# Tokens of a chunk laid out by residue modulo 16, and VectorE's 32x32 transpose for probability blocks of dilation 16 alone

## The chip, the cores and the metric

The kernel runs on one core of one Trainium2 chip. A core has five engines that each execute their own list of instructions in order: TensorE (PE in the profile, with its weight loads as PEld), VectorE (DVE), ScalarE (ACT), GpSimd (POOL) and SyncE (SP), and 16 DMA engines that move data between DRAM and on-chip memory. The metric is the device time of one execution in microseconds (us).

## The reference, cut to what matters

One decoder layer over 2048 tokens of width 1024, float32. Twelve attention heads of width 64 use a mixture of three dilated windows; two column groups of 128 go through a short gated convolution; both are concatenated, projected, normalised and added to the input.

```python
DILATED_PATTERNS = ((128, 1), (512, 4), (2048, 16))
h = rmsnorm(x, norm_pre_g)
q, k, v, g_attn, c_h, c_b, c_c, g_conv = jnp.split(h @ w_in, cuts, axis=-1)
q = rope(q, pos); k = rope(k, pos)
for window, dilation in DILATED_PATTERNS:      # keys at distance 0, d, 2d, ..., window
    o_i, lse_i = dilated_window_attn(q, k, v, window, dilation)
o = sum(softmax(lse over the three patterns) * o_i)
attn_out = o * silu(g_attn)
conv_out = c_b * causal_depthwise_conv(c_c * c_h, conv_w) * silu(g_conv)
x = x + rmsnorm(concat(attn_out, conv_out) @ w_out, norm_post_g)
```

A key that lies more than 512 tokens behind its query is seen by pattern 16 alone, so only if the distance is a multiple of 16.

## The kernel before, in words

**Tiles and stages.** The tokens are cut into four chunks of 512 (`C`). The projection's columns are eight groups of 512: group 0 and group 7 are the two convolution units, groups 1 to 6 the six head pairs. A unit is one group for one chunk, 32 units in the order group by group, chunk 0 to 3 in each. `x_chunk` (L416) loads a chunk of x (four tiles of 128 tokens by 1024), transposes it on PE (L442), splits it into a rounded float32r part and a remainder (L446, L448) and writes it to DRAM (L451); later groups read it back (`x_stream`, L475). A projection is three matmuls per 128x128x512 tile (L848 to L850). The last stage (L952 on) projects the concatenated result with w_out, reads x once more (L1043), adds, and stores (L1046).

**Order of tokens in a chunk.** Tile r of a chunk holds the tokens 4p + r, p from 0 to 127: the tokens are sorted by their residue modulo 4. So `x[rows[i]]` at L435, `x[t0, dl]` at L1043 and `out[t0, dl]` at L1046 step through DRAM by four rows, one row for each of 128 partitions.

**Attention.** `attn_unit` (L533) rotates k and q, keeps the keys of all chunks so far in `KK`, makes a second copy of q in token order (`Q1`, L582, on POOL), and transposes v on PE (L594). `v1`, the values in token order, is made through DRAM (L607, L610). Two sets of scores follow. Kind 4 (`score4`, L623) takes the patterns 4 and 16 together: for each residue r modulo 4 and each head of the pair, 128 queries against 128 keys of every chunk up to b. Kind 1 (`score1`, L648) takes pattern 1: 128 queries against 256 keys around them. VectorE adds a mask and takes the minimum (L638, L666), ScalarE exponentiates (L642, L670). `probs` (L677) takes up to four 128x128 blocks of probabilities, transposes them on PE (L684), copies them rounded from PSUM with ScalarE (L689), has VectorE form the remainder (L690), and multiplies them with the values (L703). Kind 4 of chunk b has 4(b+1) blocks for a head; of these the blocks of the chunks 0 to b-2 lie wholly more than 512 tokens back.

**Weights of the mixture.** Denominators of kind 1 go from E through DRAM into the order of kind 4 (L758, L760); the two weights are computed in small VectorE steps, squared up by one VectorE transpose (L785), written to DRAM (L788) and read back broadcast over partitions (L791). VectorE and POOL apply them (L807 to L810) and the result goes to `mix_d`.

**What sets the order.** Nothing is issued as it is written. Each operation is added to a planner (`Plan`, L111) with an engine, an assumed duration, a priority and what it reads and writes; `schedule` (L172) plays these through and fixes one static order for each engine. All DMAs go out through SP in that order. Buffers are rings of slots: five PSUM banks `st`, three `pt` slots for transposed probabilities, eight slots for x tiles, nine `xt` slots, six `xr` slots for the x rows of the last stage.

Of the kernel before, what the change touches and what calls it, by code (L numbers as in the profile page):

```python
# [40 lines left out]
def _constants():  # L42
# [9 lines left out]
    order = np.arange(C).reshape(128, 4).T.reshape(-1)  # L52
    rope[:, :, 0] = cs.transpose(1, 0, 2)[:, :, order]
    rope[:, :, 1] = sn.transpose(1, 0, 2)[:, :, order]
    q = np.arange(128)[:, None]
    k = np.arange(128)[None, :]
# [4 lines left out]
    tok = (np.arange(128) % 32) * 4 + np.arange(128) // 32  # L61
# [234 lines left out]
def hybrid_layer(ctx: ExitStack, tc: tile.TileContext, x, w_in, w_out, conv_w, g_pre, g_post,  # L296
# [27 lines left out]
    e_d = [dram.tile([4, 32, 4, 4], F32, name=f"ed{i}") for i in range(2)]  # L324
    a_d = [dram.tile([32, 4, 128], F32, name=f"ad{i}") for i in range(2)]
# [24 lines left out]
    KK = [ap_.tile([128, 4, NB * 128], F32R, name=f"kk{i}") for i in range(2)]  # L350
# [64 lines left out]

    def x_chunk(b):  # L416
# [6 lines left out]
        rows = [slice(b * C + i, (b + 1) * C, 4) for i in range(4)]  # L423
        if b == 0:

            for h in range(4):
                for g in range(2):
                    def load(h=h, g=g):
                        assert all(xn[2 * g + k].slot is xs_r[2 * g + k] for k in range(2))
                        nc.sync.dma_start(p4_r[g].ap.rearrange("p (i a) c -> p i (a c)", i=2)[:, :, h * 256:(h + 1) * 256],  # L430
                                          x[0:C].rearrange("(p i) d -> p i d", i=4)[:, 2 * g:2 * g + 2, h * 256:(h + 1) * 256])
                    add("DMA", dmat(256), -160 + 4 * h + g, load, w=[(xn[2 * g], h), (xn[2 * g + 1], h)], land=3.6)
# [62 lines left out]
    def conv_unit(n, i, b, zs):  # L495
# [16 lines left out]
        add("DVE", 0.25, pe, lambda: vec.tensor_copy(u.ap[:, 0:2, 1:], u.ap[:, 4:6, 0:127]), r=[(u, 1)], w=[(u, 2)])  # L512
# [20 lines left out]
    def attn_unit(n, p, b, zs):  # L533
# [3 lines left out]
        sl = slice(b * 128, (b + 1) * 128)  # L537

        def by_r(a):
            return a.rearrange("p (r i) -> p r i", r=4)  # L540
# [40 lines left out]
        for l in range(2):  # L581
            add("POOL", poolt(C) / 2, pr, lambda l=l: pool.tensor_copy(  # L582
                Q1.ap[:, l].rearrange("p (g r j) -> p g r j", g=4, r=4), Q.ap[:, l].rearrange("p (r g j) -> p g r j", g=4, r=4)),
                r=[(Q, l)], w=[(Q1, l)])
# [20 lines left out]
        d, dk = v_d[u % 2], ("vd", u % 2)  # L605
        for g in range(4):
            add("DMA", 0.5, pr, lambda g=g: nc.sync.dma_start(  # L607
                d[g].rearrange("(r j) c -> j r c", r=4), f(v2.ap[32 * g:32 * g + 32]).rearrange("j r k d -> j r (k d)")),
                r=[v2], w=[dk + (g,)], land=3.8)
        add("DMA", dmat(512), pr, lambda: nc.sync.dma_start(f(v1.ap), d.rearrange("g i c -> i g c")),  # L610
            r=[dk + (g,) for g in range(4)], w=[v1], land=5.0)
# [11 lines left out]
        def score4(r0):  # L623
# [3 lines left out]
            def qk():  # L627
                for r in range(r0, r0 + per):
                    for x, (i, j) in enumerate(products):
                        for h, (lo, hi) in enumerate(halves):  # L630
                            mm(ps[h].ap[:, (r - r0) * w:(r - r0 + 1) * w], Q.ap[lo:lo + 64, i, r * 128:(r + 1) * 128],  # L631
                               KK[j][lo:lo + 64, r, 0:w], start=x == 0, stop=x == 2)

# [14 lines left out]
        def score1(g0):  # L648
# [3 lines left out]
            def qk():  # L652
                for j, g in enumerate(lo):
                    k0 = b * 128 + (g - 1) * 32
# [22 lines left out]
        def probs(h, kind, blk, O):  # L677
            ps, pt = Tok(st_r), Tok(pt_r)
            m = len(blk)
            pp = P[h, kind]  # L680

            def tr():
                for i, (a, c) in enumerate(blk):
                    nc.tensor.transpose(ps.ap[:, i * 128:(i + 1) * 128], pp.ap[:, a, c * 128:(c + 1) * 128], ident)  # L684
            add("PE", 0.111 * m, pr, tr, r=[(pp, a) for a in sorted({a for a, _ in blk})] + ["cst"], w=[ps, (pt, "hold")])

            def p4():
                return ps.ap[:, :m * 128].rearrange("p (i c) -> p i c", c=128)
            add("ACT", actt(m * 128, True), pr + URG, lambda: act.copy(pt.ap[:, :m, 0, :], p4()), r=[ps], w=[(pt, 0)])  # L689
            add("DVE", dvet(m * 128), pr + URG, lambda: vec.tensor_tensor(  # L690
                pt.ap[:, :m, 1, :], p4(), f(pt.ap[:, :m, 0, :]), op=ALU.subtract), r=[ps, (pt, 0)], w=[(pt, 1)])

            def pv(part):
                for i, (a, c) in part:
                    dst = O[a // 2].ap.rearrange("p (l q) -> p l q", l=2)[:, :, (a % 2) * 128:(a % 2 + 1) * 128]
# [9 lines left out]
            for half in range(2):  # L705
                part = [(i, ac) for i, ac in enumerate(blk) if ac[0] // 2 == half]
                if part:
                    attn_last.append(add("PE", mmt(256) * len(part), pr, lambda part=part: pv(part), r=[(pt, 0), (pt, 1)] + vs, w=[O[half]]))
# [28 lines left out]
        for kind in (4, 1):  # L737
            for h in range(2):
# [7 lines left out]
                for i in range(0, len(bl), 4):  # L746
                    probs(h, kind, bl[i:i + 4], O)
# [12 lines left out]
        add("DMA", 0.5, pr, lambda: nc.sync.dma_start(  # L760
            X.ap.rearrange("p r c -> p (r c)"), ed.rearrange("g j r c -> (g j) (r c)")), r=[ek + (r,) for r in range(4)], w=[X], land=3.0)
# [14 lines left out]
        def w_b():  # L776
# [11 lines left out]
        add("DMA", 0.5, pr, lambda: nc.sync.dma_start(  # L788
            ad.rearrange("c g f -> g c f"), ar.ap.rearrange("p a b -> p (a b)")), r=[ar], w=[ak], land=2.0)
        for h in range(2):  # L790
            add("DMA", 0.73, pr, lambda h=h: nc.sync.dma_start(  # L791
                ab.ap[64 * h:64 * h + 64].rearrange("p i g f -> p (i g f)"),
                ad[2 * h:2 * h + 2].rearrange("i g f -> (i g f)").unsqueeze(0).to_broadcast([64, 1024])),
                r=[ak], w=[(ab, h)], land=8.0)


        def rows(t):
            return t.ap.rearrange("p (r g j) -> p g r j", r=4, g=4)

        def tokens(t):  # L800
            return t.ap.rearrange("p (g r j) -> p g r j", g=4, r=4)

        def weight(i):
            return ab.ap[:, i].rearrange("p g (r j) -> p g r j", r=4)

        a4, a1 = UU[4][0], UU[1][0]
        add("DVE", dvet(C), pr, lambda: vec.tensor_tensor(rows(a4), rows(a4), weight(1), op=ALU.mult), r=[ab], w=[a4], port=True)  # L807
        add("DVE", dvet(C), pr, lambda: vec.tensor_tensor(tokens(a1), tokens(a1), weight(0), op=ALU.mult), r=[ab], w=[a1], port=True)
# [306 lines left out]
```

## Time and profile before

| what | value |
|---|---|
| median of 3 runs | 1220.3 us (1217.9 to 1220.44) |
| the profiled execution | 1222.89 us |
| its span on the core | 1220.8 us |
| granted TensorE clock, mean | 0.994 |
| busy: PE, DVE, ACT, POOL | 1201.8, 916.0, 717.9, 260.1 us |
| DMA moved | 280.39 MB, 230 GB/s on average |

The span is the time from the first to the last instruction of the core; the execution's own time is 2.1 us longer. Engine busy times overlap each other. A row of the profile's groups gives line, engine, operation, output and input tile, shape, count, then the sum of busy time, the mean in ns of one, and the idle time just before it with what ended it. SPq rows are DMAs that SP issues; their duration is the issuing, not the transfer. A busy PE is one with a matmul in its pipeline: what one matmul costs is read from the distance between starts.

### The profile page before, as it was taken

The numbers are of one execution on the slowest core, as the hardware profiler recorded it, in microseconds if no ns is written. First come the engines' busy times: TensorE is split into PE (matmuls) and PEld (weight loads), VectorE is DVE, ScalarE is ACT, GpSimd is POOL, SyncE is SP. The second block draws the span as 40 slices with busy tenths as digits, with TensorE's granted clock in tenths as the row PEclk, the third lists the DMA queues.
The fourth block names the chain that finished last, engine by engine and source line by source line (L and its number), as shares of the span: only waits on it lengthen the run. The fifth ranks groups of instructions, "written<-read, shape, count | busy, mean of one in ns | idle before, by whom it ended". The sixth has DMA issues, their size and how long they took to land.

```text
span 1220.8 us, 20955 instructions
## 1 busy us (share of the span) xinstructions
PE 1201.8 (98%) x6856; PEld 993.4 (81%) x6856; DVE 916.0 (75%) x2287; ACT 717.9 (59%) x1874; POOL 260.1 (21%) x212
## 2 busy tenths in 40 slices
PE   8999999999999999999999999999999999999997
PEld 6888888888878888788887888788888888777886
DVE  5556477877777787787788867787877759988876
ACT  6533447767557676576667676486676553454443
POOL 0011123322322232222332223222323113000000
PEclk9999999999999999999999999999999999999999
DMA  9989777766777657766877748767678779555452
GB/s 342 343 317 338 269 232 236 234 205 200 240 252 245 205 182 261 240 184 209 260 223 254 243 119 269 232 234 248 199 233 280 213 229 302 174 163 175 136 181 86
DMA packets 155884, 280.39 MB, mean 230 GB/s; under 512 B 31872, under 2 KB 90368, under 8 KB 155776
## 3 DMA queue, kind: packets, MB, share of 16 engines
q1 hardware_dynamic: 155776, 279.06, 69.6%
q8 instruction: 54, 0.88, 0.3%
q14 instruction: 54, 0.44, 0.1%
HBM read 215.36 MB, written 51.05 MB: 218 GB/s over the span
## 4 chain that ended last, share of the span: by engine, by line
PE 84%; DVE 8%; DMA 3%; ACT 2%; issue 1%; SPq 1%; DVEq 0%; ACTq 0%
PE z L848 16%; PE z L850 16%; PE z L849 16%; PE st L703 8%; PE st L684 7%; PE st L631 4%; PE st L659 3%; PE st L1010 2%; PE st L1008 2%; PE st L1009 2%; DMA rp<-rp 1%; PE z L1008 1%; PE z L1010 1%; PE z L1009 1%; ACT p L642 1%
## 5 line engine op out<-in xcount | busy, mean ns | idle before, releaser
L848 PE MATMUL z<-xt,w 128*128 128x512 f32 x960 | 397.1, 414 | 0.0
L850 PE MATMUL z<-xt,w 128*128 128x512 f32 x960 | 377.7, 393 | 0.0
L849 PE MATMUL z<-xt,w 128*128 128x512 f32 x960 | 376.4, 392 | 0.0
L850 PEld LDWEIGHTS z<-xt,w 128*128 128x128 f32 x960 | 180.5, 188 | 40.3
L848 PEld LDWEIGHTS z<-xt,w 128*128 128x128 f32 x960 | 181.2, 189 | 32.7 <-issue 3.4
L849 PEld LDWEIGHTS z<-xt,w 128*128 128x128 f32 x960 | 181.5, 189 | 25.8
L690 DVE TENSOR_TENSOR pt<-st,pt 128x512 fp32r<-128x512 f32 x216 | 142.3, 679 | 48.1 <-ACT pt L689 46.2
L642 ACT ACTIVATE p<-p,sm 128x128 f32<-128x128 f32 (+3 forms) x192 | 105.9, 555 | 73.2 <-DVE sm L638 72.9
L689 ACT CAST pt<-st 128x512 fp32r<-128x512 f32 x216 | 120.0, 579 | 36.0 <-PE st L684 34.1
L703 PEld LDWEIGHTS st<-pt,v 128*128 128x128 f32 x852 | 121.5, 190 | 18.2 <-DVE pt L690 4.9
L703 PE MATMUL st<-pt,v 128*128 128x256 f32 x852 | 133.1, 287 | 2.0 <-DVE pt L690 1.9
L684 PE MATMUL st<-cst,p 128*128 128x128 f32 x852 | 123.1, 275 | 2.4 <-DVE sm L638 1.0
L723 DVE TENSOR_TENSOR uu<-st,uu 64x256 f32<-64x256 f32 x192 | 80.0, 421 | 57.1 <-ACT uu L722 53.5
L684 PEld LDWEIGHTS st<-cst,p 128*128 128x128 f32 x852 | 100.6, 141 | 22.8 <-issue 3.2
L752 POOL TENSOR_TENSOR uu<-uu 128x512 f32<-128x512 f32 x48 | 72.4, 1509 | 209.1 <-DVE uu L723 207.4
L638 DVE CUSTOM_DVE_ANT_0 p<-st,cst 128x128 f32<-128x128 f32 (+3 forms) x192 | 81.8, 487 | 46.7 <-PE st L631 46.4
L721 ACT COPY uu<-st 64x256 f32<-64x256 f32 x192 | 70.2, 368 | 58.7 <-PE st L703 52.3
L670 ACT ACTIVATE p<-p,e 128x256 f32<-128x256 f32 (+1 forms) x192 | 94.9, 499 | 12.4 <-DVE e L666 12.3
L562 POOL TENSOR_TENSOR rp<-rp,cs 128x512 f32<-128x512 f32 x24 | 35.3, 1472 | 225.7 <-DMA rp<-rp 145.4
L666 DVE CUSTOM_DVE_ANT_0 p<-st,cst 128x256 f32<-128x256 f32 (+1 forms) x192 | 66.8, 411 | 20.5 <-PE st L659 20.4
L562 DVE TENSOR_TENSOR rp<-rp,cs 128x512 f32<-128x512 f32 x72 | 55.9, 791 | 23.4 <-DMA rp<-rp 23.0
L722 ACT COPY uu<-st 64x256 f32<-64x256 f32 x192 | 69.6, 367 | 3.2 <-DVE uu L723 0.4
(320 smaller groups left out, 1842.7 us busy)
## 6 DMA issues: line engine op xcount, KB each, us to landing
xt<-xt SPq DMA_DIRECT2D x256, 512.0 KB
cs<-t SPq DMA_DIRECT2D x28, 768.0 KB
raw<-in_w_in SPq DMA_DIRECT2D x59, 256.0 KB
rp<-rp SPq DMA_DIRECT2D x192, 64.0 KB
vd<-v SPq DMA_DIRECT2D x96, 128.0 KB
v<-vd SPq DMA_DIRECT2D x24, 512.0 KB
ab<-ad SPq DMA_DIRECT2D x48, 256.0 KB
mix<-g SPq DMA_DIRECT2D x32, 256.0 KB
```

Source lines behind the costliest of these rows:

```text
L562: add(e, dur, pr, lambda o=o, a=a, i=i, eng=eng: eng.tensor_tensor(o.ap, a.ap, cs.ap[:, i], op=ALU.mult), r=[cs], w=[o], port=True)
L638: add("DVE", dvet(w) + 0.01, pr + URG, lambda h=h, r=r, P4=P4: vec.tensor_tensor_reduce(P4.ap[:, r, 0:w], ps[h].ap[:, (r - r0) * w:(r - r0 ...
L642: add("ACT", actt(w) + 0.19, pr, lambda h=h, r=r, P4=P4: act.activation(P4.ap[:, r, 0:w], P4.ap[:, r, 0:w], AF.Exp, bias=s4(0, h)[:, r:r + ...
L670: add("ACT", actt(256 - lo[g]) + 0.19, pr, lambda h=h, g=g, P1=P1: act.activation(P1.ap[:, g, lo[g]:], P1.ap[:, g, lo[g]:], AF.Exp, bias=E ...
L684: nc.tensor.transpose(ps.ap[:, i * 128:(i + 1) * 128], pp.ap[:, a, c * 128:(c + 1) * 128], ident)
L689: add("ACT", actt(m * 128, True), pr + URG, lambda: act.copy(pt.ap[:, :m, 0, :], p4()), r=[ps], w=[(pt, 0)])
L690: add("DVE", dvet(m * 128), pr + URG, lambda: vec.tensor_tensor(pt.ap[:, :m, 1, :], p4(), f(pt.ap[:, :m, 0, :]), op=ALU.subtract), r=[ps, ...
L703: mm(dst, v, pt.ap[:, i], start=s, stop=e)
L723: add("DVE", dvet(256), pr + URG, lambda: vec.tensor_tensor(cols(a, lo), o()[lo:lo + 64, 0], cols(a, lo), op=ALU.add), r=[O], w=[(a, (h, h ...
L848: mm(z.ap, w.ap[:, 0, js], xt.ap[:, 0], start=kt == 0, stop=False)
L849: mm(z.ap, w.ap[:, 0, js], xt.ap[:, 1], start=False, stop=False)
L850: mm(z.ap, w.ap[:, 1, js], xt.ap[:, 0], start=False, stop=kt == KT - 1)
```

## The change

Tile r of a chunk now holds the tokens 16a + 4s + r, at place 32s + a: within a tile the tokens are sorted by residue modulo 16, in four runs of 32. A 128x128 block of kind 4 that only pattern 16 sees then has its nonzero entries in four 32x32 squares on its diagonal. VectorE transposes such blocks in place in squares of 32 (`vec.transpose`), with no PE transpose and no PSUM bank; the ScalarE copy and VectorE remainder then read them from on-chip memory instead of PSUM. The blocks of the chunks b-1 and b go through PE as before.

All that depends on the order of tokens follows: the rope table, the masks, the reading of x, the stores of the result, the views of keys and queries, the convolution's shift (two copies where there was one), and the three detours through DRAM (v, E, the weights). Chunk 0 of x is loaded by 12 DMAs instead of 8, half of them issued by ScalarE's queue.

```diff
+    def by_place(t, b):
+        return t[b * C:(b + 1) * C].rearrange("(a s r) d -> r s a d", a=32, s=4)
...
-        rows = [slice(b * C + i, (b + 1) * C, 4) for i in range(4)]
+        rows = by_place(x, b)
...
-            for h in range(4):
-                for g in range(2):
-                    def load(h=h, g=g):
-                        nc.sync.dma_start(p4_r[g].ap.rearrange("p (i a) c -> p i (a c)", i=2)[:, :, h * 256:(h + 1) * 256],
-                                          x[0:C].rearrange("(p i) d -> p i d", i=4)[:, 2 * g:2 * g + 2, h * 256:(h + 1) * 256])
+            for h0, h1 in ((0, 1), (1, 2), (2, 4)):
+                for i, z in enumerate(xn):
+                    cols = slice(h0 * 256, h1 * 256)
+                    add("DMA", dmat(128 * (h1 - h0)), -160 + 4 * h0 + i / 2, lambda z=z, i=i, cols=cols: (act if i % 2 else nc.sync).dma_start(
+                        z.ap[:, cols], rows[i][:, :, cols]), w=[(z, h) for h in range(h0, h1)], land=3.6)
...
-                add("DMA", dmat(512), b * 100 - 160 + i, lambda z=z, i=i: nc.sync.dma_start(z.ap, x[rows[i]]), w=[(z, h) for h in range(4)])
+                add("DMA", dmat(512), b * 100 - 160 + i, lambda z=z, i=i: nc.sync.dma_start(z.ap, rows[i]), w=[(z, h) for h in range(4)])
...
-                               KK[j][lo:lo + 64, r, 0:w], start=x == 0, stop=x == 2)
+                               KK[j][lo:lo + 64, 4 * r:4 * r + 4, 0:w // 4].rearrange("p s (c a) -> p c s a", a=32), start=x == 0, stop=x == 2)
...
-                            keys = kk[:, :, k0 + 32:k0 + 64] if lo[g] else kk[:, :, k0:k0 + 64].rearrange("p r (c j) -> p c r j", c=2)
+                            keys = kk[:, :, k0 + 8:k0 + 16] if lo[g] else kk[:, :, k0:k0 + 16].rearrange("p x (c a) -> p c x a", c=2)
...
+            if far:
+                def src():
+                    return pp.ap[:, tiles[0]:tiles[-1] + 1, 0:(b - 1) * 128]
...
+                add("DVE", dvet(m * 128) + 0.05, pr, lambda: vec.transpose(src(), src()), w=[(pp, a) for a in tiles])
+                add("ACT", actt(m * 128), pr + URG, lambda: act.copy(dst(0), cut(src())), r=[(pp, a) for a in tiles], w=[(pt, 0)])
+                add("DVE", dvet(m * 128), pr + URG, lambda: vec.tensor_tensor(dst(1), cut(src()), f(dst(0)), op=ALU.subtract),
+                    r=[(pp, a) for a in tiles] + [(pt, 0)], w=[(pt, 1)], port=True)
...
+                if kind == 4 and b > 1:
+                    where = {}
+                    for half in range(2):
+                        rs = range(2 * half, 2 * half + 2)
+                        if b == 3 or half == 0:
+                            where.update(parts(h, 4, [(r, c) for r in (rs if b == 3 else range(4)) for c in range(b - 1)], True))
+                        where.update(parts(h, 4, [(r, c) for r in rs for c in (b - 1, b)]))
+                        times(h, 4, {ac: v for ac, v in where.items() if ac[0] in rs}, O[half])
...
-        for r in range(4):
-            add("DMA", 0.5, pr, lambda r=r: nc.sync.dma_start(
-                ed[:, :, r].rearrange("g j c -> j g c"), E.ap[32 * r:32 * r + 32]), r=[E], w=[ek + (r,)], land=2.9)
+        for g in range(4):
+            add("DMA", 0.5, pr, lambda g=g: nc.sync.dma_start(
+                ed.rearrange("r (s g a) c -> g (r s) a c", s=4, g=4)[g], E.ap[:, g]), r=[E], w=[ek + (g,)], land=2.9)
...
-        add("DMA", 0.5, pr, lambda: nc.sync.dma_start(
-            ad.rearrange("c g f -> g c f"), ar.ap.rearrange("p a b -> p (a b)")), r=[ar], w=[ak], land=2.0)
+        for r in range(4):
+            add("DMA", 0.5, pr, lambda r=r: nc.sync.dma_start(
+                ad[:, r].rearrange("c s a -> s c a"), ar.ap[:, r]), r=[ar], w=[ak + (r,)], land=2.0)
...
-                add("DMA", dmat(256), po - 10, lambda dl=dl, xr=xr: nc.sync.dma_start(xr.ap, x[t0, dl]), w=[xr], after=gates[1:] + streams[-1:])
+                add("DMA", dmat(256), po - 10, lambda dl=dl, xr=xr, b=b: nc.sync.dma_start(xr.ap, by_place(x, b)[i][:, :, dl]), w=[xr], after=gates[1:] + streams[-1:])
...
-                add("DMA", dmat(256), po, lambda xr=xr, dl=dl: nc.sync.dma_start(out[t0, dl], xr.ap), r=[xr])
+                add("DMA", dmat(256), po, lambda xr=xr, dl=dl, b=b: nc.sync.dma_start(by_place(out, b)[i][:, :, dl], xr.ap), r=[xr])
```

The order of each engine is planned anew, and line numbers of the changed kernel are some 3 to 33 higher. In all, PE has 144 transposes fewer (708 instead of 852), VectorE 36 in-place transposes of 512 columns more, and SP and ScalarE together issue 1,110 DMAs instead of 1,034.

On SP, at the start of the program, the kernel before stands so (a row is line, operation, output tile<-input tile, shape of the output; `p` and `uu` are x tiles, `in_w_in` the weights, `xt` the split x):

```order
L402 DMA rp_145<-in_w_in 128x512
L402 DMA g_146<-in_w_in 128x512
L826 DMA cw<-in_conv_w 128x6
L435 DMA p_187<-in_x 128x1024
L435 DMA p_188<-in_x 128x1024
L435 DMA uu<-in_x 128x1024 x2
L464 DMA cs_192<-in_rope 128x1024
L451 DMA xt_0_72<-xt_122 128x1024
```

And the changed kernel at the same place:

```order
L405 DMA rp_145<-in_w_in 128x512
L405 DMA g_146<-in_w_in 128x512
L859 DMA cw<-in_conv_w 128x6
L440 DMA p_187<-in_x 128x1x1024
L440 DMA p_188<-in_x 128x1x1024
L440 DMA uu<-in_x 128x1x1024 x2
L469 DMA cs_192<-in_rope 128x1024
L456 DMA xt_0_72<-xt_122 128x1024
```

The four loads of chunk 1 stand at the same place; their destination is written as 128 x 1 x 1024 because the source in DRAM now has two steps for the partitions, 4 outside (s) and 32 inside (a).

On SP, in the last stage, where results of the first token tiles are stored and x is read again (`out` the result, `raw` and `cs` the slots that hold x rows, `mix` the concatenated result), before:

```order
L1043 DMA raw_140<-in_x 128x512
L1046 DMA out<-cs_192 128x512 x2
L969 DMA uu<-mix_105 128x4x128 x2
L969 DMA g_148<-mix_105 128x4x128
L1043 DMA cs_192<-in_x 128x512 x2
L969 DMA uu<-mix_105 128x4x128
L1046 DMA out<-cs_192 128x512
L1046 DMA out<-raw_139 128x512
```

And the changed kernel:

```order
L1078 DMA out<-cs_192 4x32x512
L1075 DMA raw_139<-in_x 128x1x512
L1075 DMA raw_140<-in_x 128x1x512
L1002 DMA uu<-mix_105 128x4x128 x2
L1075 DMA raw_141<-in_x 128x1x512
L1002 DMA uu<-mix_105 128x4x128
L1075 DMA cs_192<-in_x 128x1x512
L1002 DMA g_148<-mix_105 128x4x128
L1078 DMA out<-cs_192 4x32x512 x2
```

The kinds of DMA and their number are the same; a store that was 128 rows by 512 is now 4 by 32 rows by 512.

More of the change, by code (lines that the diff above doesn't have):

```diff
@@ L60, in _constants @@
     four = (q - k) % 4 == 0
[L61 removed]
+    tok = np.arange(128).reshape(8, 4, 4).transpose(2, 1, 0).reshape(-1)
     tq, tk = tok[:, None], tok[None, :]
@@ L704, in probs @@
             vs = [V2[p * NB + c] for c in range(b + 1)] if kind == 4 else [V1[p * NB + c] for c in range(max(b - 1, 0), b + 1)]
[L705 to L708, printed above, removed]
+            attn_last.append(add("PE", mmt(256) * len(where), pr, pv,
+                                 r=[(pt, l) for pt in {pt for pt, _ in where.values()} for l in range(2)] + vs, w=[O]))
         UU = {}
```

104 lines of the change are left out of this document (56 added, 48 removed).

## Prediction

> **What bounds the kernel now.** I read the profile's page first, then the table by stages, then the lists of the engines in time. From the page, the span, the engines' busy time and the DMA totals:
>
> ```profile
> span 1220.8 us, 20955 instructions
> ...
> PE 1201.8 (98%) x6856; PEld 993.4 (81%) x6856; DVE 916.0 (75%) x2287; ACT 717.9 (59%) x1874; POOL 260.1 (21%) x212
> ...
> DMA packets 155884, 280.39 MB, mean 230 GB/s; under 512 B 31872, under 2 KB 90368, under 8 KB 155776
> ...
> q1 hardware_dynamic: 155776, 279.06, 69.6%
> ```
>
> PE is idle for 19 us only: work taken from it shortens the time as long as nothing else falls behind. So the second reading is which engine is next, stage by stage:
>
> ```profile
> 20.00:150.00 130.00, 130.00 (x670) 107.52 (x670) 74.47 (x180) 55.47 (x112) 15.37 (x12) 1.00 0.88 327
> 500.00:650.00 150.00, 149.15 (x925) 123.58 (x923) 115.53 (x311) 97.60 (x274) 41.82 (x34) 1.00 0.70 224
> 1100.00:1200.00 100.00, 99.74 (x428) 79.75 (x427) 82.18 (x175) 45.30 (x102) 0.00 (x0) 1.00 0.48 159
> ```
>
> The columns are window, length, busy PE, PEld, DVE, ACT, POOL, granted clock, DMA share and GB/s. In attention (500 to 650) VectorE is at 77%. From 20 to 150 us the 16 DMA engines are at 88% on average: there is nearly no room on them. In the last stage they are at 48%.
>
> **The change part by part.** *PE transposes.* One batch of eight, in PE's list:
>
> ```profile
> 664.07 0.39 PE L850 MATMUL z<-xt,w 128*128 128x512 f32 x1
> 664.30 1.04 PE L684 MATMUL st<-cst,p 128*128 128x128 f32 x8
> 665.09 0.48 PE L848 MATMUL z<-xt,w 128*128 128x512 f32 x1
> 665.41 0.39 PE L849 MATMUL z<-xt,w 128*128 128x512 f32 x1
> ```
>
> Eight hold PE for 0.79 us from start to start, and the first matmul behind them takes 0.32 us instead of the usual 0.23: 0.88 us, so 0.11 each. Chunk 2 loses 2 heads x 4 blocks, chunk 3 twice that, times six pairs: 144 transposes, **-15.8 us**, all of it on the path of a PE that is 98% busy.
>
> *VectorE and ScalarE.* The rows that price what is added:
>
> ```profile
> L638 DVE CUSTOM_DVE_ANT_0 p<-st,cst 128x512 f32<-128x512 f32 x48 | 30.4, 687 | 9.8 <-PE st L631 9.6
> ...
> L638 DVE CUSTOM_DVE_ANT_0 p<-st,cst 128x128 f32<-128x128 f32 x48 | 10.6, 287 | 2.0 <-PE st L631 1.9
> ...
> L785 DVE STREAM_TRANSPOSE t<-pa 128x128 f32<-128x128 f32 x24 | 7.5, 312 | 0.8
> ```
>
> A VectorE transpose of 128 columns takes 0.31 us; 384 more columns cost another operation 0.40 us, so one of 512 should take 0.71 us (four times 0.31, 1.25 us, at most). 36 of them are 26 us (45 at most) on an engine that has 23% to spare in that stage, 4.3 us in each pair's share of the run: 0 on the path. If that cover were gone, up to 26 us. The ScalarE copies and the remainders stay as many as before; the two small copies for the convolution and the views with short runs on POOL, which is 21% busy, I put at 0 as well.
>
> *Views of the keys.* The score matmuls stream keys in runs of 32 (kind 4) and 8 elements (kind 1), where it was whole rows and runs of 32. Twenty-four each, same width:
>
> ```profile
> 317.90 1.70 PE L631 MATMUL st<-kk,q 64*128 64x256 f32 x24
> ```
>
> ```profile
> 651.68 1.71 PE L659 MATMUL st<-kk,q 64*128 64x256 f32 x24
> ```
>
> Whole rows 1.70 us, runs of 32 1.71 us: run length has cost nothing so far, so 0. Runs of 8 are not in this trace; were they half as fast, 576 matmuls at 0.07 us would add 41 us. [...]
>
> *The DMAs of x and of the result.* Here I expect the time to be decided. A DMA whose DRAM side was a list of 128 rows now has 4 (s) outside and 32 (a) inside: 12 + 12 loads of x at the start, 32 loads and 32 stores at the end. The kernel before has one DMA of just this form, the store of the weights (L788: 4 outside, 32 inside). What its rows say:
>
> ```profile
> xt<-xt SPq DMA_DIRECT2D x256, 512.0 KB
> ...
> ed<-e SPq DMA_DIRECT2D x96, 2.0 KB
> ad<-t SPq DMA_DIRECT2D x24, 64.0 KB
> ...
> ex<-ed SPq DMA_DIRECT2D x24, 8.0 KB
> ...
> gp<-in_g_pre SPq DMA_DIRECT2D x1, 4.0 KB
> cw<-in_conv_w SPq DMA_DIRECT2D x1, 3.0 KB
> ```
>
> ```profile
> L788 SPq DMA_DIRECT2D ad<-t x24: 583/592/660, 168.3 to 1013.8; - x24
> ```
>
> ```profile
> L760 SPq DMA_DIRECT2D ex<-ed x24: 319/320/582, 159.7 to 1001.2; - x24
> ```
>
> The page counts 31,872 packets under 512 bytes. Data accounts for 96 x 128 (E, 16 bytes each), 24 x 128 (its way back) and 2 x 128 (gp, cw): 15,616. That leaves 16,256. The rows of issues, from the first quoted to the last, sum to 1,034 DMAs. If each ended with one small packet on each of 16 engines there would be 16,544; 288 fewer is 24 x 12. So 24 DMAs ended on 4 engines instead of 16, and the stores of the weights are exactly 24. SP also takes 592 ns to issue one, against 320. From this I infer that a DMA with 4 outside runs on 4 of the 16 engines; that they are the same four each time no row shows, and I assume it. [...]
>
> What one engine carries: 279.06 MB in 69.6% of 16 x 1220.8 us is 20.5 GB/s while busy; by the table, 327 / (16 x 0.88) = 23.2 in the first stage and 159 / (16 x 0.48) = 20.7 in the last.
>
> *The start.* In PE's list, the first transpose of chunk 3's x and the first score:
>
> ```profile
> 78.11 0.38 PE L442 MATMUL st<-cst,p 128*128 128x128 f32 x2
> ```
>
> ```profile
> 139.95 1.56 PE L631 MATMUL st<-kk,q 64*128 64x128 f32 x24
> ```
>
> The first score follows chunk 3's first transpose by 61.8 us of dense PE work, and the changed PE list has the same work between them. Each of the four engines must carry a quarter of all 8.4 MB of x, 2.1 MB, at 23.2 GB/s 90 us. Ahead of chunk 3's last load stand, in SP's list, the weights of group 0, twelve writes of `xt`, tables and constants, 11.7 MB over 16 engines: 32 us more. Chunk 3 is there at 0.7 + 90 + 32 = 123 us, the first score at 185 instead of 140: **+45 us**. Ends: at 20.5 GB/s +61; if nothing but x stood in those queues, 153 us, +13.
>
> *The end.* Stores in SP's list, the first and two later ones:
>
> ```profile
> 1074.69 1.01 SPq L1046 DMA_DIRECT2D out<-raw x2
> ...
> 1173.71 5.20 SPq L1046 DMA_DIRECT2D out<-cs x3
> ...
> 1193.22 1.00 SPq L1046 DMA_DIRECT2D out<-raw x2
> ```
>
> Half a chunk takes 19.5 us (1173.71 to 1193.22), which is PE's pace. It needs four loads and four stores of 256 KB, 65.5 KB on each of four engines: 8 x 2.8 us at 23.2 GB/s, 8 x 3.2 at 20.7, and 3 us for the four loads of `mix`, which use all sixteen: 26 to 28 us. So the four engines become the bound. From the first store on, 59 of the 64 DMAs and 28 loads of `mix` are left: 187 to 209 us, end at 1262 to 1284 instead of 1221: +41 to +63, I take **+52**, the middle, as the packets of x are longer than the stage's mean. If the queues also run dry while SP, which issues in order, waits at a load whose slot is still being stored, 1.5 us per half chunk more: +75.
>
> *The other detours* are 16-byte or 128-byte runs, or 16 outside. The weights' store is four DMAs instead of one, 1.8 us more of SP's time, in front of what SP issues next (k and q's rotation, `xt`). VectorE waited for the weights once, 1.4 us (the columns: total, times, longest):
>
> ```profile
> DVE uu L807 <- DMA ab<-ad: 1.4, 1, 1.4
> ```
>
> I put **+2**; were it on the path at every chunk 3, 6 x 1.8 = 11.
>
> **Sum.** The profiled execution took 1222.9 us (span 1220.8 and 2.1 around it), 2.6 more than the median of the three runs. 1222.9 - 15.8 + 45 + 52 + 2 = 1306, against the median **1303**. Ends: 1222.9 - 15.8 + 13 + 41 = 1261 and 1222.9 - 15.8 + 61 + 75 + 11 = 1354.
>
> **The rivals.** *All engines after all* (faster): the load and the store of x are spread over 16 engines, or over four different ones at a time. Then the transposes' gain stands: 1222.9 - 15.8 + 2 = 1209, 1206 against the median. For it: only small DMAs of this form are in the trace, no load among them. Against: the count is exact, and the form is the same. It decides from eight engines on: x is then there at 0.7 + 45 + 32 = 78 us, when PE wants it, and half a chunk of the end needs 14 us, under 19.5. *One end hidden* (slower): the four engines bind at one end only, because the loads of the start overlap better or the slots of the end run far enough ahead: 1222.9 - 15.8 + 2 + 45 or 52 = 1254 or 1261. *Short runs* (slower): DMAs as before, but PE reads runs of 8 at half rate: 1222.9 - 15.8 + 2 + 41 = 1250.
>
> **How the numbers follow.** Forecast 0.68, one end 0.16, all engines 0.11, short runs 0.04, and 0.01 for effects that cancel. The range from 1245 to 1345 holds the first two rivals on the slow side and the forecast but for its last few us; it leaves out the faster case. About 0.2% is what a measurement of this kernel can tell from no change: faster 0.11, same 0.01, slower 0.88.
>
> **What would show it.** PE busy falls by some 15 us, 36 VectorE transposes take about 0.7 us. In the first stage PE stands idle before L447 with x's DMA as releaser, and the first score comes near 185 us. Small packets fall short of 16 for each DMA by 12 for every load and store of x. Stores of the last stage come 26 to 28 us apart. I am wrong if x's transposes do not wait, or half a chunk still takes 19.5 us.

## The result and the profile after

The changed kernel takes 1312.2 us (median of 6 runs, 1308.3 to 1315.1), the kernel before 1220.7 beside it: a ratio of 1.0751, 95% interval 1.0729 to 1.0773. The forecast was 1303. From the page of the changed kernel, the span, the busy time, PE and its clock in slices, and the packets:

```profile
span 1306.5 us, 20808 instructions
...
PE 1206.0 (92%) x6712; PEld 992.1 (76%) x6712; DVE 923.9 (71%) x2331; ACT 718.8 (55%) x1874; POOL 262.3 (20%) x212
...
PE   4686999999999999999999999999999999799784
...
PEclk6797999999999999999999999999999999999898
...
DMA packets 173102, 280.39 MB, mean 215 GB/s; under 512 B 52672, under 2 KB 107072, under 8 KB 172992
```

PE was idle for 19 us and is idle for 100 now, nearly all of it in the first four slices and the last six. The table by stages (columns as in the prediction) says the same, with attention (500 to 650) nearly as full as it was:

```profile
0.00:20.00 20.00, 6.67 (x26) 5.20 (x26) 2.27 (x7) 3.07 (x4) 0.20 (x4) 0.72 0.32 106
20.00:150.00 130.00, 95.74 (x435) 77.44 (x436) 52.81 (x125) 45.70 (x78) 7.21 (x6) 0.85 0.62 230
...
500.00:650.00 150.00, 147.74 (x912) 122.78 (x912) 118.05 (x325) 97.97 (x272) 41.46 (x35) 1.00 0.77 234
1100.00:1200.00 100.00, 86.06 (x350) 67.58 (x349) 66.49 (x141) 38.70 (x84) 0.85 (x1) 0.95 0.38 122
1200.00:1306.00 106.00, 75.46 (x300) 57.46 (x298) 57.83 (x127) 31.35 (x72) 0.00 (x0) 0.90 0.33 109
```

From 20 to 150 us PE does 435 matmuls instead of 670, while the DMA engines are busy for 62% on average instead of 88%: a kernel that waits for transfers, on DMA engines that are on average less loaded than before. That fits a few overloaded engines among idle ones.

**The count.** Data account for 12,288 small packets of E, 12,288 on its way back (24 x 512 now), 12,288 of the weights and 256 of gp and cw: 37,120. Of 52,672 that leaves 15,552, and 1,110 DMAs with 16 each would be 17,760: short by 2,208 = 184 x 12. (Packets of 4 bytes in the trace: 15,553, and 16,257 in the kernel before.) The DMAs with 4 outside are 96 stores of the weights, 24 loads, 32 reloads and 32 stores: 184.

**The start.** PE's waits over the whole execution (total us, times, longest):

```profile
PE st L447 <- DMA p<-in_x: 15.9, 5, 5.8
PE st L447 <- DMA uu<-in_x: 9.2, 2, 4.6
PE z L881 <- DVE rp L511: 9.1, 1, 9.1
PE z L881 <- DVE u L512: 7.7, 2, 3.9
```

and the first score, in PE's list (it was at 139.95):

```profile
L641 PE MATMUL st<-kk,q x24: 269/272/326, 193.1 to 194.4; 64*128 64x128 f32 x24
```

The waits for x are those of chunks 0 and 1; the last of them ends at 55.73 us. The waits for VectorE are waits for x too, at two removes. In the waits of the stretch from 100 to 119 us ScalarE stands still for x:

```profile
ACT ab L459 <- DMA p<-in_x: 13.6, 2, 9.7
ACT ab L459 <- DMA uu<-in_x: 5.2, 1, 5.2
```

and VectorE, in its list, stands behind ScalarE:

```profile
109.90 0.75 DVE L453 SCALAR_TENSOR_TENSOR xt<-st,gp,xt 128x512 fp32r<-128x512 f32 x1 [12.79 <-ACT xt L451]
110.57 0.68 DVE L511 TENSOR_TENSOR rp<-z,cs 128x512 f32<-128x512 f32 x1
```

L459 sums the squares of chunk 3's x. Behind it in ScalarE's order stand copies of chunk 2's transposes (L451), behind those VectorE's remainders (L453) and the convolution's step (L511) that frees the bank PE wants at L881. PE had no need of chunk 3 yet: it transposes it from 131.3 us on. The loads of chunk 3, in SP's list of the kernel after, go out at 92.8 us:

```profile
92.79 1.18 SPq L440 DMA_DIRECT2D p<-in_x  x2
```

and before at 49.0:

```profile
49.02 1.44 SPq L435 DMA_DIRECT2D p<-in_x  x2
```

In both kernels the DMA directly ahead of these loads in SP's list is a store of the convolution's result (L533, before L527). SP stands there until VectorE has made it, and issues it here at 92.4 us (before at 48.3), the loads right behind it. So the loads run one chunk after the other, and each lateness is handed on.

Behind this stop PE is slower as well. In its list, two matmuls before the stop of 9.1 us at L881 and two behind it:

```profile
101.03 0.39 PE L881 MATMUL st<-xt,w 128*128 128x512 f32 x1
101.27 0.39 PE L882 MATMUL st<-xt,w 128*128 128x512 f32 x1
...
112.39 0.63 PE L883 MATMUL z<-xt,w 128*128 128x512 f32 x1
112.81 0.63 PE L881 MATMUL z<-xt,w 128*128 128x512 f32 x1
```

From start to start they take 0.24 us before the stop and 0.42 to 0.43 us for some 10 us behind it. The granted clock is 1.00 from 90 to 102 us and 0.69 from 112 to 121.

**The end.** The first store, and the last group of four, which begins at 1290.6 us, in SP's list:

```profile
1115.22 4.07 SPq L1078 DMA_DIRECT2D out<-raw  x3
...
1290.60 1.26 SPq L1078 DMA_DIRECT2D out<-cs  x2
```

Seven half chunks in 1290.6 - 1115.2 are 25.1 us each, where 19.7 stood before ((1212.7 - 1074.7) / 7). From the first store to the end of the span it takes 191 us, was 146: +45. What the compute engines wait for there is not x. It is the loads of `mix`, the concatenated result; from the waits of the kernel after and of the kernel before, over the whole execution:

```profile
DVE uu L931 <- DMA uu<-mix: 39.9, 8, 8.3
```

```profile
DVE w L977 <- DMA uu<-mix: 0.3, 1, 0.3
```

These loads are written as they were. VectorE's sums and ScalarE's rounding of `mix` come late by them, and PE behind those. That they come late because a part of each lies on the four engines behind x and the result is inferred; it fits with the runs below, where this wait falls to 6.0 us with every DMA of x and the result split.

### The profile page after: what moved, and what is told of

Read it like the earlier page. It is cut to its first block, busy times and chain, and to the rows that moved or that the text cites. A ratio compares the mean times of both kernels' runs of the same rounds, so it can differ in the third digit from the quotient of the medians.

```text
span 1306.5 us, 20808 instructions
## 1 busy us (share of the span) xinstructions
PE 1206.0 (92%) x6712; PEld 992.1 (76%) x6712; DVE 923.9 (71%) x2331; ACT 718.8 (55%) x1874; POOL 262.3 (20%) x212
## 2 busy tenths in 40 slices
DMA packets 173102, 280.39 MB, mean 215 GB/s; under 512 B 52672, under 2 KB 107072, under 8 KB 172992
## 4 chain that ended last, share of the span: by engine, by line
PE 62%; DMA 17%; DVE 12%; ACT 3%; issue 3%; SPq 1%; DVEq 0%; ACTq 0%
PE z L881 13%; PE z L883 13%; PE z L882 13%; PE st L731 6%; PE st L709 5%; DMA uu<-mix 4%; DMA p<-in_x 3%; DMA uu<-in_x 3%; PE st L641 3%; PE st L669 2%; DMA ed<-e 1%; DMA out<-raw 1%; DVE p L648 1%; PE st L881 1%; DVE w L413 1%
## 5 line engine op out<-in xcount | busy, mean ns | idle before, releaser
L881 PE MATMUL z<-xt,w 128*128 128x512 f32 x960 | 397.6, 414 | 16.7 <-DVE rp L511 9.1
L881 PEld LDWEIGHTS z<-xt,w 128*128 128x128 f32 x960 | 182.4, 190 | 55.0 <-issue 15.5
L731 PEld LDWEIGHTS st<-pt,v 128*128 128x128 f32 x852 | 117.5, 190 | 13.9 <-DVE pt L715 2.9
L731 PE MATMUL st<-pt,v 128*128 128x256 f32 x852 | 124.8, 285 | 1.0 <-DVE pt L715 1.0
L715 DVE TENSOR_TENSOR pt<-st,pt 128x512 fp32r<-128x512 f32 (+1 forms) x180 | 117.1, 675 | 10.9 <-ACT pt L714 9.7
L714 ACT CAST pt<-st 128x512 fp32r<-128x512 f32 (+1 forms) x180 | 98.8, 579 | 17.6 <-PE st L709 16.2
L709 PE MATMUL st<-cst,p 128*128 128x128 f32 x708 | 99.2, 274 | 0.9 <-DVE uu L749 0.8
L791 POOL TENSOR_TENSOR uu<-uu 128x512 f32<-128x512 f32 x48 | 66.9, 1393 | 139.1 <-DVE uu L749 129.5
L709 PEld LDWEIGHTS st<-cst,p 128*128 128x128 f32 x708 | 82.5, 140 | 14.7 <-DVE uu L749 2.1
```

What stands on the lines that cost most here:

```text
L731: mm(dst, v, pt.ap[:, i], start=s, stop=e)
L881: mm(z.ap, w.ap[:, 0, js], xt.ap[:, 0], start=kt == 0, stop=False)
```

## The experiments

The theory: a DMA with 4 outside runs on 4 engines, and that costs both ends. Rivals: the permuted order of rows, runs of 8 in the keys, or VectorE's new work. Each run is set against the kernel before, measured beside it: 1219.4 to 1219.5 us.

**Every DMA of x and of the result in four of 32 partitions.**

```diff
+    def quarters(eng, dst, src, load):
+        for s in range(4):
+            if load:
+                eng.dma_start(dst[32 * s:32 * s + 32], src[s])
+            else:
+                eng.dma_start(dst[s], src[32 * s:32 * s + 32])
-                add("DMA", dmat(512), b * 100 - 160 + i, lambda z=z, i=i: nc.sync.dma_start(z.ap, rows[i]), w=[(z, h) for h in range(4)])
+                add("DMA", dmat(512), b * 100 - 160 + i, lambda z=z, i=i: quarters(nc.sync, z.ap, rows[i], True), w=[(z, h) for h in range(4)])
...
```

> The changed kernel, with every load and reload of x and every store of the result written as four DMAs of 32 partitions each (32 rows outside, where one DMA had 4 outside and 32 inside); the plan of the rest is unchanged. Theory (a DMA with 4 outside runs on 4 of the 16 engines, and nothing else costs much): x is there when TensorE wants it, the first score comes near 125 to 130 us instead of 193, half a chunk of the end takes 19 to 20 us instead of 25.1, and the time is 1222.9 - 15.8 + 3.6 (runs of 8 in the keys) = 1211, with 264 more DMAs on SP's list 1205 to 1225. Rival (the wait for x comes from how rows are permuted, from short runs in the keys or from VectorE's transposes, not from the number of engines): the time stays between 1290 and 1315.

Measured: 1224.1 us, ratio to before 1.0042 (1.0025 to 1.0058). 88 of the 92 us are gone, with the same rows in the same order at the same places. The rival falls. Its page:

```profile
span 1219.9 us, 21164 instructions
...
PE 1190.4 (98%) x6712; PEld 985.8 (81%) x6712; DVE 925.2 (76%) x2331; ACT 718.9 (59%) x1874; POOL 261.4 (21%) x212
```

But 1211 was expected, and two things in that were wrong. First, the first score comes at 150.0, not at 125 to 130: before it was at 140, and TensorE's own work, not x, sets that. In the first 60 us PE is busy 6.7 us less than in the kernel before (48.6 against 55.2). Second, from the first store on PE is idle for 11.7 us, not 7.8. Waits for VectorE at the scores appear too, at L677:

```profile
PE st L677 <- DVE sm L656: 4.0, 2, 3.2
```

But between the first score and the first store PE is idle for 6.4 us in all, as before (6.5): they stand in place of other waits. So PE is busy 11.4 us less and idle 10.5 us more: 6.7 at the start and 3.9 from the first store on, 2 of these behind the last matmul (the last stores are eight DMAs to issue).

**The start alone, the end alone.** The same edit at L436 and L440 only, and at L1075 and L1078 only.

> The changed kernel, only the 24 loads of x at the start written as four DMAs each. Theory: the start's share alone goes. The first score falls from 193 us to 125 to 130, of which 53 us stand against the kernel before; the last stage stays at about 25 us per half chunk. Time 1312 - 53 = 1259, 1245 to 1268. Rival (one of the two ends carries the whole loss, the other is an echo of a plan that runs late): either 1312 as before, or under 1230.

> The changed kernel, only the 32 reloads of x and the 32 stores of the result in the last stage written as four DMAs each. Theory: the end's share alone goes. The first score stays at 193 us, half a chunk of the end falls from 25.1 to 19 to 20 us. Time 1312 - 45 = 1267, 1255 to 1280. Rival (the end is slow because SP needs longer for each DMA, or since what stands before the stores has become late): more DMAs on SP's list then leave half a chunk at 24 us or more, and the time at 1300 or over.

Measured: 1268.2 us (ratio 1.0402, 1.0376 to 1.0429) and 1266.2 (1.0383, 1.036 to 1.0406): the start gives back 44, the end 46, the two together 88 (1.3 us less each when every time is set against the kernel before beside it). The first is 0.2 over the range that I gave, since the first score comes at 149.9 here too: of the 53 us lost at the start, the split loads leave 10. The ends are independent and each carries half. Where only the start is mended, half a chunk still takes 25.5 us, in SP's list:

```profile
1071.74 4.07 SPq L1086 DMA_DIRECT2D out<-raw  x3
...
1250.22 1.25 SPq L1086 DMA_DIRECT2D out<-cs  x2
```

(1250.2 - 1071.7) / 7 = 25.5. Where only the end is mended it takes 19.8, though SP has 192 DMAs more to issue:

```profile
1115.72 5.51 SPq L429 DMA_DIRECT2D out<-raw  x12
...
1254.37 3.62 SPq L429 DMA_DIRECT2D out<-cs  x8
```

**The addressing alone, put into the kernel before.**

```diff
+    def by_place(t, b):
+        return t[b * C:(b + 1) * C].rearrange("(a s r) d -> r s a d", a=32, s=4)
-                add("DMA", dmat(512), b * 100 - 160 + i, lambda z=z, i=i: nc.sync.dma_start(z.ap, x[rows[i]]), w=[(z, h) for h in range(4)])
+                add("DMA", dmat(512), b * 100 - 160 + i, lambda z=z, i=i: nc.sync.dma_start(z.ap, by_place(x, b)[i]), w=[(z, h) for h in range(4)])
...
```

> The kernel before, with nothing of the change but the addressing of x and of the result: loads, reloads and stores go through views with 4 outside and 32 inside. The tokens are permuted by that, so that the output is not the reference's; all instructions on the other engines stay as they are. Theory: this alone costs what the change lost at both ends, 53 + 45 us, so 1221 + 98 = 1319, 1295 to 1335, the first score near 190 to 200 us and 24 to 28 us per half chunk. Rival (the transposes, the short runs or VectorE's new work bring the loss): 1221, at most 1230.

Measured: 1325.0 us, ratio 1.087 (1.0845 to 1.0895): +106 with nothing else of the change, 13 more than the changed kernel, which has the shorter PE list. The first score comes here:

```profile
L636 PE MATMUL st<-kk,q x24: 268/272/327, 195.2 to 196.5; 64*128 64x128 f32 x24
```

**The same with 8 outside and 16 inside, and with 16 and 8.** The first of the two, against the run with 4:

```diff
-        return t[b * C:(b + 1) * C].rearrange("(a s r) d -> r s a d", a=32, s=4)
+        return t[b * C:(b + 1) * C].rearrange("(a s r) d -> r s a d", a=16, s=8)
```

> The kernel before with x and the result addressed through views with 8 outside and 16 inside (before with 4 outside and 32 inside: 1325, which is 106 over); tokens permuted, so the output is not the reference's; the other engines' instructions as before. Theory (such a DMA runs on as many engines as it has rows outside): with eight, x is there at about 0.7 + 45 + 32 = 78 us, as TensorE wants it, and half a chunk of the end needs 13 to 14 us of them, under the 19.5 of TensorE. So nearly the whole loss goes: 1222 to 1235. Rival one (the permuted rows themselves are slow to read and write): 1315 to 1330. Rival two (the loss falls in proportion to the engines): 1265 to 1280.

> The kernel before with x and the result addressed through views with 16 outside and 8 inside (with 4 and 32: 1325, with 8 and 16: 1241); tokens permuted, so the output is not the reference's. Theory (as many engines as rows outside, up to all 16): the small packets are again 16 for each DMA, start and end are those of the kernel before but for the eight DMAs more with which chunk 0 is loaded: 1219 to 1228. Rival (the form with two levels of rows costs of itself, beside the number of engines): what the run with 8 lost at the start, some 14 us, stays: 1232 to 1242.

Measured: 1240.7 us (ratio 1.0174, 1.0156 to 1.0192) and 1225.7 (1.0062, 1.0043 to 1.008). By the number outside the loss is 106, 21 and 6 us: the form with two levels of rows costs little in itself. The small packets, 31,872 before, are these, of the run with 4, the one with 8 and the one with 16:

```profile
DMA packets 154908, 280.38 MB, mean 212 GB/s; under 512 B 30896, under 2 KB 89392, under 8 KB 154800
```

```profile
DMA packets 155276, 280.38 MB, mean 226 GB/s; under 512 B 31264, under 2 KB 89760, under 8 KB 155168
```

```profile
DMA packets 156012, 280.39 MB, mean 230 GB/s; under 512 B 32000, under 2 KB 90496, under 8 KB 155904
```

All three have 8 DMAs more than the kernel before, 128 packets. With 16 outside it is exactly those. With 4 and 8 the 92 DMAs (28 loads, 32 reloads, 32 stores) fall short by 12 and by 8 each: 31,872 + 128 - 1,104 = 30,896 and 31,872 + 128 - 736 = 31,264. So by the count the number of engines is the number of rows outside, for 4, 8 and 16. With 32 outside it is 16: the run with the end alone in four has 56,512 small packets, 52,672 + 64 x (4 x 16 - 4). With eight the end is mended, 19.8 us per half chunk ((1229.55 - 1090.77) / 7), but not the start, where my expectation missed:

```profile
L636 PE MATMUL st<-kk,q x24: 268/272/327, 159.1 to 160.4; 64*128 64x128 f32 x24
```

19 us late. I had let all of x flow from the beginning; a chunk's loads stand behind earlier work in SP's order, as above. On half the engines each would also take about twice as long as on sixteen, an estimate at the same rate for each engine; no run separates the two. With sixteen the first score comes at 142.9, 3 us late.

**The transposes back on PE, with every DMA in four.** The True asks for VectorE:

```diff
-                            where.update(parts(h, 4, [(r, c) for r in (rs if b == 3 else range(4)) for c in range(b - 1)], True))
+                            where.update(parts(h, 4, [(r, c) for r in (rs if b == 3 else range(4)) for c in range(b - 1)]))
```

> The changed kernel with all DMAs of x and the result in four (1224 us), and its far probability blocks again transposed by TensorE, as in the kernel before; no VectorE transposes. Theory (the transposes' gain is there on TensorE's list and was spent elsewhere): 144 transposes of 0.11 us come back, 1224 + 16 = 1240, 1232 to 1244. Rival (VectorE's 26 us of transposes cost TensorE in waits what they save): 1224, at most 1229.

Measured: 1234.7 us (ratio 1.0127, 1.0111 to 1.0143). PE is busy for 1205.3 us against 1190.4: 14.9 for 144 transposes, 0.10 each. The spans of the profiled executions differ by 13.1 (1233.0 against 1219.9), so that 1.8 of the 14.9 went into idle time. The medians differ by 10.6 only, but the run with VectorE's transposes spreads from 1220.6 to 1229.6. The wait at L677 above is not among PE's waits in this run; another for VectorE, at L739, is 3.7 us, where it was 1.1.

**Rows of stride 4 again, the residue order made on the chip.** PE's transposes of x write PSUM in natural order, the copies out of PSUM read it by residue, and the last stage's rounding steps read the mixed values back in natural order. The second run has the far blocks on PE besides.

```diff
-                    nc.tensor.transpose(ps.ap[:, i * 128:(i + 1) * 128], xn[i].ap[:, kt * 128:(kt + 1) * 128], ident)
+                    nc.tensor.transpose(laid(ps.ap, i), xn[i].ap[:, kt * 128:(kt + 1) * 128], ident)
-                s.ap[:, 0], ps.ap, AF.Copy, scale=gp[:, kt:kt + 1]), r=[ps, "gp"], w=[(s, 0)])
+                placed(s.ap[:, 0]), sorted_(ps.ap), AF.Copy, scale=gp[:, kt:kt + 1]), r=[ps, "gp"], w=[(s, 0)])
-            add("ACT", actt(C), pr, lambda: act.copy(view(m, 0), cells(t)), r=[t], w=[(m, 0)])
+            add("ACT", actt(C), pr, lambda: act.copy(rows4(view(m, 0)), natural(t)), r=[t], w=[(m, 0)])
...
```

> The changed kernel with x and the result in rows of stride 4 again, 128 rows outside, as in the kernel before; the tokens are put into residue order on the chip (TensorE's transposes of x write PSUM in natural order and the copies out of it read it by residue; the last stage reads the mixed values by residue in its two forms). Theory: start and end are those of the kernel before, TensorE's list is shorter by 15.8 - 3.6 = 12 us, and 2 us of new waits in the attention stage remain as in the run with every DMA in four: 1220 - 10 = 1210, 1204 to 1216. Rival (the views by residue cost ScalarE and VectorE more than their slack, or the gain is lost to waits on VectorE): 1218 to 1235.

> The same kernel with rows of stride 4 and residue order made on the chip, but the far blocks transposed by TensorE. Theory: 16 us more than with VectorE's transposes, and 4 to 6 more than the kernel before (runs of 8 in the keys and the views by residue): 1224 to 1230. Rival: as with VectorE's transposes, within 3 us.

Measured: 1226.9 us (ratio 1.0066, 1.0043 to 1.0089) and 1241.2 (1.0178, 1.0161 to 1.0196). VectorE's transposes are worth 14.3 us here, near the 16 expected, but both runs are some 11 us above their ranges: of the first run the rival held, that the views by residue cost more than the slack. The place is the last stage, 163 us from the first store on instead of 146. ScalarE's rounding step there, in the kernel with rows of stride 4:

```profile
L1029 ACT CAST xt<-uu 128x512 fp32r<-128x512 f32 x29 | 32.3, 1137 | 28.7 <-DVE uu L945 28.7
```

and in the kernel before:

```profile
L976 ACT CAST xt<-uu 128x512 fp32r<-128x512 f32 x28 | 16.6, 615 | 18.5 <-DVE uu L898 18.5
```

Reading elements that lie 128 bytes apart in on-chip memory takes ScalarE 1137 ns here instead of 615, and PE waits for the ScalarE copies queued behind it (5.6 us in all at `PE st L1061 <- ACT rp L1068`, three more waits like it). VectorE's remainders behind it (L1030) take 1113 ns instead of 687. At the start a like view costs nothing; there ScalarE reads PSUM, elements 64 bytes apart:

```profile
L465 ACT ACTIVATE xt<-st,gp 128x512 fp32r<-128x512 f32 x32 | 21.8, 685 | 35.8 <-PE st L461 35.7
```

against 686 ns before.

**Both halves that worked.** The start of that kernel, the end in DMAs of 32 partitions, and the very last store issued by ScalarE:

```diff
-                add("DMA", dmat(256), po, lambda xr=xr, dl=dl, b=b: quarters(nc.sync, by_place(out, b)[i][:, :, dl], xr.ap, False), r=[xr])
+                add("DMA", dmat(256), po, lambda xr=xr, dl=dl, b=b, e=act if (q, i, j) == (7, 2, 1) else nc.sync: quarters(e, by_place(out, b)[i][:, :, dl], xr.ap, False), r=[xr])
```

> The changed kernel with VectorE's transposes kept, loads of x in rows of stride 4 with residue order made on the chip (as in the kernel that does this at both ends), reloads and stores of the last stage in four DMAs of 32 partitions each (as in the kernel that splits all), and the very last store issued from ScalarE's queue. Theory: the start's 7 us that the split loads lost against the kernel before come back, and 2 us at the last stores: 1224 - 8 = 1216, 1211 to 1219, against 1219 of the kernel before. Rival (on VectorE's and ScalarE's side the views by residue at the start cost as much): 1222 to 1227.

Measured: 1210.7 us, ratio 0.9937 (0.9924 to 0.995): faster than both kernels, by 8.8 us against before, and 0.3 under the range expected. From its page:

```profile
span 1207.9 us, 21037 instructions
...
PE 1185.3 (98%) x6712; PEld 981.3 (81%) x6712; DVE 923.3 (76%) x2331; ACT 719.6 (60%) x1874; POOL 262.9 (22%) x212
```

The first score comes at 137.7 us; half a chunk takes 19.8 us ((1197.07 - 1058.16) / 7). The gain came by other shares than expected. Against the run with every DMA in four the start is 12 us earlier, not 7, and the store moved to ScalarE brought nothing: the span ends 9.7 us behind the last matmul, where it was 9.1 (7.0 in the kernel before).

**Runs of 8 and of 4 in the keys, in the kernel before.**

```diff
-                            keys = kk[:, :, k0 + 32:k0 + 64] if lo[g] else kk[:, :, k0:k0 + 64].rearrange("p r (c j) -> p c r j", c=2)
+                            keys = kk[:, :, k0 + lo[g] // 4:k0 + 64].rearrange("p r (a j) -> p a r j", j=8)
```

> The kernel before, with the kind 1 scores reading the same keys in runs of 8 elements in place of 32 (the keys of a score come in another order, so the output is not the reference's); nothing else is changed. Theory (runs of 8 cost TensorE what the changed kernel's rows show): 24 matmuls take 1.79 us in place of 1.64, PE's busy time in that line grows by 3.6 to 4 us, and the time by as much: 1219 + 4 = 1223, 1221 to 1225. Rival (runs of 8 are free, as the prediction had it, and the longer rows of the changed kernel come from its order of tokens): 1219, at most 1220.5.

> The same with runs of 4 elements. If each run's beginning has a price (512 runs of 8 per 24 matmuls cost 0.15 us more than a quarter as many): runs of 4 cost about twice as much more, 24 matmuls some 2.0 us, and the time is 1219 + 8 to 10 = 1228. [...]

Measured: runs of 8 1219.5 us (ratio 0.9999, 0.9987 to 1.0011), runs of 4 1221.5 (1.0025, 1.0014 to 1.0037). The rows of the kind 1 scores, in the kernel before, then with runs of 8, with runs of 4, and in the changed kernel:

```profile
L659 PE MATMUL st<-kk,q 64*128 64x256 f32 x540 | 40.0, 290 | 0.0
```

```profile
L659 PE MATMUL st<-kk,q 64*128 64x256 f32 x540 | 39.7, 288 | 0.0
```

```profile
L659 PE MATMUL st<-kk,q 64*128 64x256 f32 x540 | 44.4, 308 | 0.0
```

```profile
L669 PE MATMUL st<-kk,q 64*128 64x256 f32 x540 | 44.3, 305 | 4.8 <-DVE sm L648 4.8
```

My theory falls: a run of 8 costs nothing by itself, a run of 4 costs 4.4 us of PE in all. The changed kernel pays 4.3 with runs of 8, so its price comes from something else in its view (sixteen runs 512 bytes apart, where the test had four 2,048 apart). Which, no run tells.

## Why the prediction was right

*PE transposes, -15.8.* Right: 14.9 us of PE's busy time, 0.10 each, in the pair with the DMAs in four, and 17.6 in the pair with rows of stride 4 (1207.9 against 1190.3). In time it is 10.6 and 14.3.

*VectorE and ScalarE, 0 on the path, one transpose 0.71 us.* The size was right, from the list of groups of the kernel after:

```profile
L700 DVE STREAM_TRANSPOSE p<-p 128x512 f32<-128x512 f32 x36 | 24.2, 697 | 8.5 <-ACT p L652 8.5
```

The price was near 0: PE waits for VectorE at the scores (4.8 us at L669 in the kernel after), but between the first score and the first store its idle time grew by 1.4 us only, from 6.5 to 7.9.

*Runs of 8, 0.* Runs of 8 alone cost 0 (288 ns per matmul against 290), as the rows of longer runs suggested. That the new view of the keys costs nothing did not follow: 4.3 us. Runs of 4 alone take 18 ns more per matmul (308 against 290).

*The start, +45.* The four engines were right, and the size: +53 at the first score. The step "chunk 3 is there at 123 us, the first score at 185" came out by another way. ScalarE's last wait for chunk 3's x ends at 120.1, near the 123, but not because the loads flowed from the beginning: they went out chunk by chunk, the last from 92.8 on. That the arrival agrees is luck. PE was not ready for it, as the sum had taken it to be. It had lost time at chunks 0 and 1 and behind ScalarE's early need of chunk 3, and transposes chunk 3 from 131.3 on, the same 61.8 us ahead of the first score. Those are the 8 us that the sum lacks. It also had no term for a slower PE. The same 656 matmuls up to the first score keep PE busy for 145.5 us, where it was 135.2, at a mean granted clock of 0.87 instead of 0.99: 10 of the 53. Not all of that need be the clock; with the loads split they take 138.6 us at 1.00.

*The end, +52.* Mechanism right, size a little over: +45. Half a chunk takes 25.1 us, not 26 to 28. The packets of 2,048 bytes, which from 1116 to 1290 us are those of x and the result, moved 14.03 MB in 629.6 us of packet time, 22.3 GB/s, between the two rates of the sum (the packets of 512 bytes, those of `mix`, 18.2), and 53.5 of those DMAs, not 56, went by in the seven half chunks. On four engines that is 157 us of the 174; a sixteenth of the 332 us of `mix` adds 21. So the four were busy all the while, and SP's waits did not add to it. The sum did not say who would wait: it is VectorE, for `mix`, 39.9 us. With one end split at a time the ends measure 44 and 46, against 97 forecast for both.

*The other detours, +2.* Not seen: VectorE's wait for the weights, 1.4 us before, is not among the waits of the kernel after.

*The rivals.* "All engines after all" is out by the count and by the run with the DMAs in four; its time, 1206, is near what the best version reaches. "One end hidden" is out by the two runs of one end each. "Short runs" is out by its own run. That the four engines are the same ones each time is in no row, but the packets of the trace show it. In the last stage SP issues up to four stores within some 5 us. If each ran on four engines of its own, more than four packets would be under way at a time. From 1116 to 1290 us those of 2,048 bytes are four or five at a time in 73% of the time and six or more in under 1%; in the kernel before, from 1075 to 1213 us, sixteen and more are under way in 14% of it.

*The sum.* By the spans, the first score comes 53.1 us later, the stretch from there to the first store is 12.6 shorter (922.1 against 934.7), and what follows is 45.2 longer: +85.7, 1306.5 - 1220.8. Forecast were +45, -13.8 (the transposes and the detours) and +52, together +83. So the mechanism held at both ends, but that the sum came so close is partly luck: the start was 8 short and the end 7 over.

## What to carry to other kernels

Before a row order is changed, read what the new DRAM view has outermost: a DMA here used as many engines as that number, up to 16 (by the count 4, 8 and 16, and 16 with 32 outside), at 16 KB as at 512. The average busy share hid it (62% from 20 to 150 us); the count of small packets showed it (2,208 short), and splitting the DMA along the outer dimension gave the engines back (1224.1 us instead of 1312.2). The permutation cost nothing here where ScalarE read PSUM (685 against 686 ns for 512 columns), and half a microsecond where it read on-chip memory at 128 bytes from element to element (1137 against 615 ns).

## What had not been expected

- The granted clock was lower where PE stood idle: 0.85 from 20 to 150 us and 0.95 from 1100 to 1200, where both were 1.00. So the waits for data were paid twice here: with the same list PE is busy for 1206.0 us in the changed kernel and for 1190.4 with the DMAs split.
- At the end the compute engines wait for a transfer that was not changed (`mix`, 39.9 us instead of 0.3).
- A step of one engine that waited early for data (ScalarE's sum of squares) held up another that didn't need them: PE stood for 9.1 us at L881 behind chunk 3's x, two engines away.
- Reading by residue was free out of PSUM (685 against 686 ns on ScalarE for 512 columns, 64 bytes apart) and took nearly twice as long out of on-chip memory (1137 against 615, 128 bytes apart).
- SP issued a store of the result in 0.54 to 0.58 us with 4 outside, in 0.34 with 128 rows, and a quarter of one in 0.42 (medians): the 264 more DMAs of the quarters left half a chunk at PE's pace and cost 2 us behind the last matmul.
